# Two more Strassen pairs in each half of both down projections, and what is moved to make room for them

## The chip, the core and the metric

The kernel runs on one core of one Trainium2 chip. The core has a matrix engine (TensorE, PE in the profile), three engines for elementwise work (VectorE or DVE, ScalarE or ACT, GpSimd or POOL, the last unused here) and the SyncE queue (SP), which issues nearly every DMA. The metric is the device time of one execution in microseconds; the median of several runs counts. The profile is of one execution.

## The reference, cut to what matters

```python
# two layers; x is 256 tokens x 2048, all float32; D_FF = 5632
h = rms_norm(x, p['mix_pre'])
m = mixer(h)                                   # attention, differs by layer
x = x + rms_norm(m, p['mix_post'])
h = rms_norm(x, p['ffn_pre'])
x = x + rms_norm(conv_glu(h, *p['ffn']), p['ffn_post'])

def rms_norm(x, g):
    return x * lax.rsqrt(jnp.mean(x * x, axis=-1, keepdims=True) + 1e-6) * g

def conv_glu(h, w_up, conv_w, conv_b, w_down):
    u = h @ w_up                               # 2048 -> 2 x 5632
    gate, val = u[..., :D_FF], u[..., D_FF:]
    gate = depthwise_conv3(gate, conv_w, conv_b)
    return (gelu(gate) * val) @ w_down         # 5632 -> 2048
```

The change touches the channel mixer (`conv_glu`) of both layers and the norm behind it.

## The kernel before

**Products.** TensorE takes operands in a rounded 32-bit format (`fp32r`). To keep float32 accuracy every operand is split into a high part, rounded, and a low part, the rest. A weight chunk is 128 x 1024 (512 KB). It is loaded into a buffer `raw` by SP, its high part `whi` is cast by ScalarE (L157 in `_split`), its low part `wlo` is subtracted by VectorE (L152). A product is high x high, high x low and low x high, three matmuls. `weights()` hands out the chunks in the order of one list for the whole program (`all_chunks`). Of `whi` and `wlo` there are five buffers each, of `raw` four, and `self.more` can name other free tiles that serve as further raw buffers (`raw_more`).

**Stages of the channel mixer** (`ffn`). The up projection runs over eleven groups `gi` of 512 gate columns (`pg`) and 512 value columns (`pv`), eight chunks each. The pre-norm's factor per token, `r`, is not applied to the input but to the results: `self.rb` holds it for all tokens, gates are multiplied by it in `gates`, values by L1140. The product of the gated activation and the value is split into `gh[gi]`, `gl[gi]`. The last group's pair is called `g_last`.

**Down projection** (`down`). Output columns are cut into two halves `h` of 1024. The 5632 rows are 22 pairs of 256. A pair is a 2 x 2 block product (two row blocks, two column blocks, two token blocks of 128). A "plain" pair computes its eight block products, in two chunks of four. A "seven" pair uses Strassen's scheme (Winograd's form): seven block products from sums of weight blocks and sums of token blocks, in units `j` = 0 to 3 that have 2, 2, 2 and 1 products. Units 0 and 3 read the weights as they are (512 KB and 256 KB), units 1 and 2 read sums of weight blocks.
- `PAIRS` says how many of the 22 pairs of each half are "seven": 9 and 11 in both layers.
- `down_order` writes the order of units: `LEAD` plain chunks first, then the seven pairs, with a plain chunk wherever its tuple has `None`, then the plain chunks that are left.
- `block_sums` makes the weight sums during the up projection: it loads a pair's 1 MB from `w_down`, subtracts on VectorE (L1151) and stores the result to DRAM (`self.blocks`), one pair per 7 ticks.
- `sums` makes the token sums of the seven pairs when the down projection begins: five additions on VectorE (L1183) and a split (L692 on ScalarE, L693 on VectorE) for one pair, or for two at once. Results live in tiles that are free by then (`homes`). Both halves use the same token sums.
- `x` is needed again only by the residual, so it is stored (`kept`) in the up projection and loaded back by `x_back` at the end of half 1.
- `done` and `three` make the sums of squares for the norm behind; `crossing` (layer 0) or `tail` (layer 1) ends the stage. The last five plain chunks of half 1 (`HELD`) run first for token block 0, then for block 1, so that the norm of block 0 overlaps with products.

**What sets the order.** A generator such as `block_sums` or `sums` is a background task: `tick()` runs one step of each, and it is called once per chunk. The program so written is then put in order per engine by the scheduler of the framework, which adds the waits; an engine executes in that order. SP, too, is one queue: a DMA that waits for a buffer holds up those behind it.

Of the kernel before, what the change touches and what calls it, by code (L numbers as in the profile page):

```python
# [34 lines left out]

PAIRS = (9, 11), (9, 11)
LEAD = 5, 1


def down_order(h, pairs):

    plain = [("plain", p, o) for o in range(2) for p in range(pairs, KF // 2)]
    out, plain = plain[:LEAD[h]], deque(plain[LEAD[h]:])
    for p in range(pairs):
        for j in (0, None, 1, 2, 3) if h and p > 2 else (0, None, 1, 2, None, 3):
            out.append(plain.popleft() if j is None else ("seven", p, j))
    return out + list(plain)

# [8 lines left out]
class Model:  # L59
# [288 lines left out]
    def pre_norm(self, sp=None):  # L348

        nc = self.nc  # L350
        yield
        ss = self.small.tile([P, 2, 4], F32, tag="ss", name="ss", bufs=2)
        for c in range(4):
            while self.led <= 2 * c:
                yield
            for t in range(2):
                with self.behind(self.gate):
                    self.square_sums(ss[:, t, c:c + 1], self.x[c][:, t, :])
            yield
# [71 lines left out]
        self.nc.sync.dma_start(out=gb, in_=self.a["post"][post:post + 1, 512 * c:512 * c + 512].broadcast_to([P, 512]))  # L431
        return gb

    def three(self, ss):

        part = self.col("part", 2)
        self.nc.vector.tensor_reduce(out=part, in_=ss[:, :, 0:3], op=ALU.add, axis=AX.X)
        self.nc.vector.tensor_scalar(out=part, in0=part, scalar1=1.0 / D, scalar2=EPS, op0=ALU.mult, op1=ALU.add)
        return part

    def factor(self, t, sums, part, after=()):
# [648 lines left out]
    def ffn(self, layer, pre):  # L1090
        nc, tc = self.nc, self.tc
        with tc.tile_pool(name=f"ffn{layer}", bufs=1) as sp:
            self.room = sp
            xs = self.xhl
            x = lambda k: xs[k // 4][:, k % 4].rearrange("p a t -> p (a t)")
            gh = [sp.tile([P, 4, T], F32R, tag=f"gh{i}", name=f"gh{i}") for i in range(NFG - 1)]
            gl = [sp.tile([P, 4, T], F32R, name=f"gl{i}") for i in range(NFG - 1)]
# [5 lines left out]
            blocks = None  # L1103
            for gi in range(NFG):
                if gi == 1:
                    kept = self.dram.tile([4, P, 2, 512], F32, name=f"x_kept{layer}")
                    for c in range(4):
                        nc.sync.dma_start(out=kept[c], in_=self.x[c])
                    blocks = self.now(self.block_sums(layer, sp))
# [19 lines left out]

                if gi:  # L1130
                    gates()
                pv = self.proj_t(KD, x, "at", after=None if gi else gates)
                if gi == NFG - 1:
                    self.finish(blocks)
                    both = sp.tile([P, 2, 4, T], F32R, tag="g_last", name="g_last", bufs=1)
                    gh.append(both[:, 0])
                    gl.append(both[:, 1])
                for i in range(4):
                    u = self.joined(gw[:, 2 + i % 2], misc[:, 2 + i % 2], pv[i])
                    nc.vector.tensor_tensor(out=u, in0=u, in1=self.rb, op=ALU.mult)  # L1140
                    nc.vector.tensor_tensor(out=u, in0=u, in1=act[:, i], op=ALU.mult)
                    self.parted(gh[gi][:, i, :], gl[gi][:, i, :], u)
            self.down(gh, gl, 2 * layer + 1, pre, kept)

    def block_sums(self, layer, sp):

        nc, w = self.nc, self.a[f"w_down{layer}"]
        jobs = [(h, p) for h in range(2) for p in range(PAIRS[layer][h])]

        def minus(x, a, b, n=512):  # L1150
            nc.vector.tensor_tensor(out=x[:, a:a + n], in0=x[:, b:b + n] if n > 512 else x[:, a:a + n],  # L1151
                                    in1=x[:, a:a + n] if n > 512 else x[:, b:b + n], op=ALU.subtract)

        def half(x, i):
            return x[:, 1024 * i:1024 * i + 1024]

        old = None
        for n in range(len(jobs) + 1):
            job, new = (jobs[n] if n < len(jobs) else None), None
            for q in range(7):  # L1160
                if job and q == 0:
                    new = sp.tile([P, 2048], F32, tag=("st", "g_last")[n % 2], name="blocks", bufs=1)
                if job and q < 2:
                    nc.sync.dma_start(out=half(new, q), in_=half(w[job[0], job[1]], q))
                if old and q == 1:
                    with self.behind([self.low]):
                        minus(old[1], 512, 1024, 1024)
                if old and q == 2:
                    with self.behind([self.low]):
                        minus(old[1], 1536, 512)  # L1170
                        minus(old[1], 0, 1536)
                    kept = self.blocks[layer, *old[0]] = self.dram.tile([P, 2048], F32, name=f"b{layer}{old[0][0]}_{old[0][1]}")
                if old and q in (3, 4):
                    nc.sync.dma_start(out=half(kept, q - 3), in_=half(old[1], q - 3))
                    if q == 4 and not job:
                        return
                yield
            old = (job, new)

    def down(self, gh, gl, post, pre, kept):  # L1180

        nc = self.nc
        add = lambda out, a, b, op=ALU.add: nc.vector.tensor_tensor(out=out, in0=a, in1=b, op=op)  # L1183
        mm = nc.tensor.matmul
        ss = self.small.tile([P, 2, 4], F32, tag="ss", name="ss", bufs=2)
        seven, m, gains = [], [], []
        many = PAIRS[0 if pre else 1]

        homes = [(self.act, "x0", 1), (self.act, "x1", 1), (self.act, "xm0", 2), (self.act, "xm1", 2),
                 (self.act, "xm2", 2), (self.room, "st", 2), (self.room, "gw", 1)]  # L1190
        self.more = [(self.act, "x2"), (self.room, "yf"), (self.act, "x3"), (self.room, "misc")]

        def x_back():
            for c in range(4):
                self.x[c] = self.act.tile([P, 2, 512], F32, name=f"x{c}")
                nc.sync.dma_start(out=self.x[c], in_=kept[c])

        def sums(upto, small=False):

            while len(seven) < upto:  # L1200
                p = len(seven)
                pool, tag, q = homes.pop(0)
                k = slice(2 * (p % 2), 2 * (p % 2) + 2 * q)
                if small:
                    tmp = self.wp.tile([P, 2, 512], F32, tag="raw", name="sums", bufs=4)
                else:
                    tmp = self.act.tile([P, 2, 512 * q], F32, tag="xm3", name="sums")
                add(tmp[:, 0], gh[p // 2][:, k].rearrange("p k t -> p (k t)").bitcast(F32),
                    gl[p // 2][:, k].rearrange("p k t -> p (k t)").bitcast(F32))
                a = tmp[:, 0].rearrange("p (q k t f) -> p q k t f", q=q, k=2, t=2)  # L1210
                s = tmp[:, 1].rearrange("p (q n f) -> p q n f", q=q, n=4)
                a11, a12, a21, a22 = (a[:, :, k, t] for t in range(2) for k in range(2))
                add(s[:, :, 0], a21, a22)
                add(s[:, :, 1], s[:, :, 0], a11, ALU.subtract)
                add(s[:, :, 2], a11, a21, ALU.subtract)
                add(s[:, :, 3], a12, s[:, :, 1], ALU.subtract)
                yield
                home = pool.tile([P, q, 4, 2, P], F32R, tag=tag, name=f"seven{p}")
                self.parted(home[:, :, :, 0, :], home[:, :, :, 1, :], s)
                seven.extend(home[:, i] for i in range(q))  # L1220
                yield

        def tokens(k, t):
            return tuple(g[k // 4][:, k % 4, t * P:(t + 1) * P] for g in (gh, gl))
# [44 lines left out]
                yield  # L1269

        gains.append(self.gain_row(post, 0))
        self.now(sums(many[0]))
        ended = None
        for h in range(2):
            items = down_order(h, many[h])
# [46 lines left out]
            if h == 0:  # L1322
# [152 lines left out]
```

## Time and profile before

| | us |
|---|---|
| median of 3 runs | 2039.87 (2039.24 to 2040.02) |
| the profiled execution | 2040.39 |
| its span, first to last instruction | 2038.6 |
| up projection, layer 0 and layer 1 | 342.5 to 820.0, 1326.4 to 1803.8 |
| down projection, layer 0 and layer 1 | 820.1 to 1047.1, 1804.0 to 2029.9 |
| VectorE busy in the up projections | 376 and 377 of 477 |
| VectorE busy in the down projections | 179 of 224 and 178 of 226 |
| DMA share in the same four stages | 0.82, 0.84, 0.82, 0.80 |
| TensorE clock granted | 0.999 |

A line of a group reads: line of the kernel, engine, operation, tiles written and read, shape, count; busy time and mean duration of one; idle time before them and what ended it. Matmuls overlap in the pipeline, so their durations add up to more than the time that passes; the distance from start to start is what one of them takes of the stage. In the table by windows a row has the stretch, the busy time of each engine with its number of instructions, the granted clock, the share of the DMA engines that was busy, and GB/s.

### The profile page before, as it was taken

The page shows a single profiled execution, that of the slowest core. Times are in us where ns is not written, and L with a number is a line of the kernel's source. Part 1 is how long each engine was busy: PE and PEld are TensorE (multiplying, and loading weights), DVE is VectorE, ACT ScalarE, POOL GpSimd, SP SyncE. Part 2 cuts the span into 40 slices and gives each one's busy share as a digit, 9 for nine tenths or more (in the row PEclk, how much of TensorE's full clock was granted, in tenths as well). Part 3 has the DMA queues.
Part 4 walks back from the last instruction along what each step waited for, and adds up shares of the span by engine and source line. Part 5 has one row for each costly group of instructions (what it writes and reads, how often), then busy time and mean ns, then how long its engine had stood idle before and what let it go on. Part 6 is the DMA issues. An engine that isn't in the chain of part 4 may idle for free.

```text
span 2038.6 us, 29774 instructions
## 1 busy us (share of the span) xinstructions
PE 2026.6 (99%) x10882; PEld 1740.7 (85%) x10882; DVE 1562.0 (77%) x2388; ACT 1161.4 (57%) x1817; POOL 0.2 (0%) x4
## 2 busy tenths in 40 slices
PE   9999999999999999999999999999999999999998
PEld 7888888888888888888878998888888888888886
DVE  6877757887887787967787875678887887788777
ACT  7655546655555555656665665565555555566664
POOL 0000000000000000000000000000000000000000
PEclk9999999999999999999999999999999999999999
DMA  9545567788888886788964445688878879768895
GB/s 336 177 152 165 166 196 237 237 312 294 289 314 294 288 293 216 247 292 282 319 220 161 140 128 172 204 277 279 302 272 322 298 278 318 235 200 307 269 318 200
DMA packets 145586, 509.75 MB, mean 250 GB/s; under 512 B 16160, under 2 KB 16672, under 8 KB 145440
## 3 DMA queue, kind: packets, MB, share of 16 engines
q1 hardware_dynamic: 145152, 507.58, 73.9%
q8 instruction: 85, 1.39, 0.3%
q14 instruction: 61, 0.50, 0.1%
q10 hardware_dynamic: 288, 0.28, 0.0%
HBM read 459.55 MB, written 48.23 MB: 249 GB/s over the span
## 4 chain that ended last, share of the span: by engine, by line
PE 98%; DVE 1%; ACT 1%; DMA 1%; issue 0%; DVEq 0%; SPq 0%; ACTq 0%
PE ps L234 31%; PE ps L236 16%; PE ps L219 8%; PE ps L217 8%; PE ps L218 8%; PE ps L1298 7%; PE ps L1299 7%; PE ps L1301 7%; PE ps L644 2%; PE ps L303 1%; PE ps L547 1%; DMA raw<-in_w_in 1%; PE ps L474 0%; PE ps L554 0%; ACT whi L157 0%
## 5 line engine op out<-in xcount | busy, mean ns | idle before, releaser
L152 DVE TENSOR_TENSOR wlo<-raw,whi 128x1024 fp32r<-128x1024 f32 (+1 forms) x655 | 784.3, 1205 | 352.2 <-ACT whi L157 344.3
L157 ACT CAST whi<-raw 128x1024 fp32r<-128x1024 f32 (+1 forms) x655 | 676.8, 1037 | 565.6 <-PE ps L234 280.1
L234 PE MATMUL ps<-xhl,whi 128*128 128x512 f32 x2752 | 952.6, 394 | 0.0
L236 PE MATMUL ps<-xhl,wlo 128*128 128x256 f32 x2752 | 757.5, 277 | 0.0
L234 PEld LDWEIGHTS ps<-xhl,whi 128*128 128x128 f32 x2752 | 513.9, 188 | 117.3
L236 PEld LDWEIGHTS ps<-xhl,wlo 128*128 128x128 f32 x2752 | 516.4, 188 | 2.6
L152 DVE TENSOR_TENSOR wlo<-raw_more,whi 128x1024 fp32r<-128x1024 f32 (+1 forms) x125 | 140.3, 1137 | 55.1 <-ACT whi L157 51.1
L1298 PE MATMUL ps<-whi,gh 128*128 128x512 f32 x440 | 171.3, 389 | 0.0
L1299 PE MATMUL ps<-whi,gl 128*128 128x512 f32 x440 | 171.2, 389 | 0.0
L157 ACT CAST whi<-raw_more 128x1024 fp32r<-128x1024 f32 (+1 forms) x125 | 121.5, 984 | 83.5 <-PE ps L1299 69.3
L1301 PE MATMUL ps<-wlo,gh 128*128 128x512 f32 x440 | 138.7, 389 | 0.0
L217 PE MATMUL ps<-whi,xhl 128*128 128x512 f32 x336 | 132.4, 395 | 0.8 <-ACT whi L157 0.8
L218 PE MATMUL ps<-wlo,xhl 128*128 128x512 f32 x336 | 131.3, 391 | 0.0
L219 PE MATMUL ps<-whi,xhl 128*128 128x512 f32 x336 | 131.0, 391 | 0.1
L1151 DVE TENSOR_TENSOR blocks<-blocks 128x512 f32<-128x512 f32 (+1 forms) x120 | 103.7, 864 | 0.7
L217 PE MATMUL ps<-whi,oh 128*128 128x512 f32 x256 | 100.3, 392 | 0.0
L218 PE MATMUL ps<-wlo,oh 128*128 128x512 f32 x256 | 99.7, 390 | 0.0
L219 PE MATMUL ps<-whi,ol 128*128 128x512 f32 x256 | 99.7, 389 | 0.0
L1298 PEld LDWEIGHTS ps<-whi,gh 128*128 128x128 f32 x440 | 82.6, 188 | 17.6 <-DVE ps L1183 0.4
L1301 PEld LDWEIGHTS ps<-wlo,gh 128*128 128x128 f32 x440 | 82.6, 188 | 17.1
L1299 PEld LDWEIGHTS ps<-whi,gl 128*128 128x128 f32 x440 | 82.6, 188 | 17.0
L307 ACT COPY gw<-ps 128x256 f32<-128x256 f32 x176 | 64.4, 369 | 46.0 <-PE ps L234 28.8
(231 smaller groups left out, 2333.6 us busy)
## 6 DMA issues: line engine op xcount, KB each, us to landing
raw<-in_w_up SPq DMA_DIRECT2D x352, 512.0 KB, 5.1
raw<-in_w_in SPq DMA_DIRECT2D x84, 512.0 KB, 4.2
blocks<-in_w_down SPq DMA_DIRECT2D x80, 512.0 KB, 6.0
b<-blocks SPq DMA_DIRECT2D x80, 512.0 KB, 5.6
raw<-in_w_down SPq DMA_DIRECT2D x77, 512.0 KB, 5.3
raw<-in_w_out SPq DMA_DIRECT2D x64, 512.0 KB, 4.1
raw_more<-in_w_down SPq DMA_DIRECT2D x59, 512.0 KB, 5.7
raw<-b SPq DMA_DIRECT2D x42, 512.0 KB, 5.9
```

The costliest lines, as they stand in the source:

```text
L152: return nc.vector.tensor_tensor(out=lo[:, s], in0=raw[:, s], in1=hi[:, s].bitcast(F32), op=ALU.subtract)
L157: self.nc.scalar.copy(hi[:, s], raw[:, s])
L217: mm(ps, lh, rh, start=start, stop=False)
L218: mm(ps, lh, rl, start=False, stop=False)
L219: return mm(ps, ll, rh, start=False, stop=stop)
L234: ins = mm(out[i], hi[:, s[kk]], x(k), start=k == 0, stop=False, skip_group_check=opening)
L236: ins = mm(out[i][:, :T], lo[:, s[kk]], x(k)[:, :T], start=False, stop=k == nk - 1, skip_group_check=opening)
L307: self.nc.scalar.copy(b, ps[:, T:])
L1151: nc.vector.tensor_tensor(out=x[:, a:a + n], in0=x[:, b:b + n] if n > 512 else x[:, a:a + n], in1=x[:, a:a + n] if n > 512 else x[:, b:b + ...
L1298: mm(bank, xh, w[0][:, c], start=start, stop=False, skip_group_check=loose)
L1299: mm(bank, xl, w[0][:, c], start=False, stop=False, skip_group_check=loose)
L1301: ins = mm(bank, xh, w[1][:, c], start=False, stop=stop, skip_group_check=loose)
```

## The change

The numbers of seven pairs rise from 9 and 11 to 11 and 13, in both layers, and with them the rules of `down_order`. The weight sums start half a group earlier and take 6.8 ticks per pair. The token sums of the first four pairs are made in the up projection, into `x0` to `x3`; eight pairs follow when the down projection starts, the thirteenth in half 1. Three tiles serve as `raw_more`, not four. The values are no longer multiplied by `r`: the norm behind is invariant to a factor per token but for its epsilon, which is multiplied by `v`, the inverse square of that factor (`floor`).

```diff
-PAIRS = (9, 11), (9, 11)
-LEAD = 5, 1
+PAIRS = (11, 13), (11, 13)
+LEAD = 4, 1
+DENSE = (4, 6, 7, 8, 9, 10), (4, 6, 8)
...
     for p in range(pairs):
-        for j in (0, None, 1, 2, 3) if h and p > 2 else (0, None, 1, 2, None, 3):
+        for j in (0, None, 1, 2, 3) if h == 0 and p in DENSE[0] else (0, 1, 2, 3) if p in DENSE[1] and h else \
+                (0, None, 1, 2, 3) if h else (0, None, 1, 2, None, 3):
             out.append(plain.popleft() if j is None else ("seven", p, j))
...
+        self.floor = self.col("floor", 2)
+        nc.vector.tensor_scalar(out=self.floor, in0=v, scalar1=EPS, scalar2=None, op0=ALU.mult)
...
-    def three(self, ss):
+    def three(self, ss, floor=None):
...
+            self.nc.vector.scalar_tensor_tensor(out=part, in0=part, scalar=1.0 / D, in1=floor,
+                                                op0=ALU.mult, op1=ALU.add)
...
+            homes = [(self.act, f"x{c}", 1) for c in range(4)] + [(self.act, f"xm{c}", 2) for c in range(3)] + \
+                [(sp, "st", 2), (self.act, "x0", 1)]
+            sums = lambda upto, *tmp: self.token_sums(seven, homes, gh, gl, upto, *tmp)
             for gi in range(NFG):
+                if gi == 2:
+                    early = self.now(sums(4, sp, "gh9"))
...
-                    nc.vector.tensor_tensor(out=u, in0=u, in1=self.rb, op=ALU.mult)
...
+        todo = {}
+        for n, (h, p) in enumerate(jobs):
+            for at, step in ((0, "load0"), (1, "load1"), (7, "sums"), (8, "keep0"), (9, "keep1")):
+                todo.setdefault(n * 34 // 5 + at, []).append((step, h, p, n))
...
+    def token_sums(self, seven, homes, gh, gl, upto, room, room_tag, bufs=1, pause=6):
...
+            seven.extend(home[:, i] for i in range(q))
+            for _ in range(pause):
+                yield
...
-        homes = [(self.act, "x0", 1), (self.act, "x1", 1), (self.act, "xm0", 2), (self.act, "xm1", 2),
-                 (self.act, "xm2", 2), (self.room, "st", 2), (self.room, "gw", 1)]
-        self.more = [(self.act, "x2"), (self.room, "yf"), (self.act, "x3"), (self.room, "misc")]
+        self.more = [(self.room, t) for t in ("yf", "gw", "misc")]
...
-        self.now(sums(many[0]))
+        self.now(sums(12, self.act, "xm3"))
...
+                if h and i == units[20]:
+                    self.now(sums(many[1], self.wp, "raw", 4))
...
-                self.now(sums(many[1], True))
-        part = self.three(ss)
+        part = self.three(ss, self.floor)
```

Three places show how instructions move.

On TensorE, pair 9 of half 0 in layer 0 is plain before. This is the first of its two chunks, the first of the down projection: token block 0, then block 1, each two products of three matmuls (`gh_3124` and `gl_3134` are `gh[4]` and `gl[4]`, whose last two of four rows are the pair; x2 is two in a row).

```order
L1298 MATMUL ps<-whi,gh_3124 128x512
L1299 MATMUL ps<-whi,gl_3134 128x512
L1298 MATMUL ps<-whi,gh_3124 128x512
L1299 MATMUL ps<-whi,gl_3134 128x512
L1301 MATMUL ps<-wlo,gh_3124 128x512 x2
L1298 MATMUL ps<-whi,gh_3124 128x512
L1299 MATMUL ps<-whi,gl_3134 128x512
L1298 MATMUL ps<-whi,gh_3124 128x512
L1299 MATMUL ps<-whi,gl_3134 128x512
L1301 MATMUL ps<-wlo,gh_3124 128x512 x2
```

Now the same pair is a seven pair further back in half 0. These are its units 2 and 3 (`seven_8306` holds the token sums of pairs 8 and 9).

```order
L1312 MATMUL ps<-whi,seven_8306 128x512
L1313 MATMUL ps<-whi,seven_8306 128x512
L1312 MATMUL ps<-whi,seven_8306 128x512
L1313 MATMUL ps<-whi,seven_8306 128x512
L1315 MATMUL ps<-wlo,seven_8306 128x512 x2
L1312 MATMUL ps<-whi,seven_8306 128x512
L1313 MATMUL ps<-whi,seven_8306 128x512
L1315 MATMUL ps<-wlo,seven_8306 128x512
```

A plain chunk is 12 matmuls and a pair 24; units 0 to 2 are 6 matmuls and unit 3 is 3, a pair 21.

On VectorE, at the start of layer 0's down projection before: token sums of pairs 2 to 5 stand between the splits of the weights.

```order
L1183 TENSOR_TENSOR sums<-gh_3121,gl_3131 128x1024
L152 TENSOR_TENSOR wlo<-raw_more,whi 128x1024
L1183 TENSOR_TENSOR sums<-sums 128x2x128 x3
L152 TENSOR_TENSOR wlo<-raw_more,whi 128x512
L1183 TENSOR_TENSOR sums<-sums 128x2x128
L152 TENSOR_TENSOR wlo<-raw_more,whi 128x1024
L693 TENSOR_TENSOR seven_8144<-sums,seven_8144 128x8x128
L152 TENSOR_TENSOR wlo<-raw,whi 128x1024
L1183 TENSOR_TENSOR sums<-gh_3122,gl_3132 128x1024
L152 TENSOR_TENSOR wlo<-raw,whi 128x1024
```

Now, at the same place: the sums of pairs 6 to 9 (pairs 0 to 3 have been made in the up projection, 4 and 5 just before these rows).

```order
L1198 TENSOR_TENSOR sums<-gh_3125,gl_3134 128x1024
L1198 TENSOR_TENSOR sums<-sums 128x2x128
L154 TENSOR_TENSOR wlo<-raw_more,whi 128x1024
L1198 TENSOR_TENSOR sums<-sums 128x2x128 x3
L154 TENSOR_TENSOR wlo<-raw_more,whi 128x1024
L154 TENSOR_TENSOR wlo<-raw_more,whi 128x512
L701 TENSOR_TENSOR seven_8207<-sums,seven_8207 128x8x128
L1198 TENSOR_TENSOR sums<-gh_3126,gl_3135 128x1024
L154 TENSOR_TENSOR wlo<-raw,whi 128x1024 x2
L1198 TENSOR_TENSOR sums<-sums 128x2x128
```

The start of the stage keeps four double sums; the two single ones that stood ahead of them are gone.

On SP, at the end of half 1 in layer 0, before: `x0` and `x1` are back already, the last plain chunks are loaded, then `x2` and `x3`, then the last held chunk and the next stage's weights.

```order
L135 DMA raw_more_9630<-in_w_down0 128x512
L135 DMA raw_more_9642<-in_w_down0 128x1024
L135 DMA raw_more_9660<-in_w_down0 128x1024
L135 DMA raw_9715<-in_w_down0 128x1024
L135 DMA raw_9727<-in_w_down0 128x1024
L135 DMA raw_9747<-in_w_down0 128x1024
L135 DMA raw_9759<-in_w_down0 128x1024
L1196 DMA x2_9739<-x_kept0_3681 128x1024
L1196 DMA x3_9741<-x_kept0_3681 128x1024
L135 DMA raw_9779<-in_w_down0 128x1024
L135 DMA raw_9819<-in_w_in1 128x1024
```

Now all four loads of `x` stand here. `x0` is the home of the thirteenth pair, so its load waits for that pair's last matmul.

```order
L137 DMA raw_more_9690<-in_w_down0 128x512
L137 DMA raw_9708<-in_w_down0 128x1024
L137 DMA raw_9747<-in_w_down0 128x1024
L137 DMA raw_9765<-in_w_down0 128x1024
L137 DMA raw_9777<-in_w_down0 128x1024
L1235 DMA x1_9787<-x_kept0_3689 128x1024
L1235 DMA x2_9789<-x_kept0_3689 128x1024
L1235 DMA x3_9791<-x_kept0_3689 128x1024
L137 DMA raw_9797<-in_w_down0 128x1024
L1235 DMA x0_9785<-x_kept0_3689 128x1024
L137 DMA raw_9809<-in_w_down0 128x1024
L137 DMA raw_9829<-in_w_down0 128x1024
```

The last three held chunks are behind loads of `x`, where only the last one was.

More of the change, by code (lines that the diff above doesn't have):

```diff
@@ L432, in gain_row @@
         return gb
-    def three(self, ss):
+    def three(self, ss, floor=None):
         part = self.col("part", 2)
         self.nc.vector.tensor_reduce(out=part, in_=ss[:, :, 0:3], op=ALU.add, axis=AX.X)
-        self.nc.vector.tensor_scalar(out=part, in0=part, scalar1=1.0 / D, scalar2=EPS, op0=ALU.mult, op1=ALU.add)
+        if floor is None:
+            self.nc.vector.tensor_scalar(out=part, in0=part, scalar1=1.0 / D, scalar2=EPS, op0=ALU.mult, op1=ALU.add)
+        else:
+            self.nc.vector.scalar_tensor_tensor(out=part, in0=part, scalar=1.0 / D, in1=floor,
+                                                op0=ALU.mult, op1=ALU.add)
         return part
@@ L1131, in ffn @@
                     gates()
+                else:
+                    blocks = self.now(self.block_sums(layer, sp))
                 pv = self.proj_t(KD, x, "at", after=None if gi else gates)
@@ L1137, in ffn @@
                     gl.append(both[:, 1])
+                elif gi == NFG - 2:
+                    for g, n in ((gh, "gh"), (gl, "gl")):
+                        g.append(sp.tile([P, 4, T], F32R, tag=f"{n}{gi}", name=f"{n}{gi}", bufs=1))
                 for i in range(4):
                     u = self.joined(gw[:, 2 + i % 2], misc[:, 2 + i % 2], pv[i])
-                    nc.vector.tensor_tensor(out=u, in0=u, in1=self.rb, op=ALU.mult)
                     nc.vector.tensor_tensor(out=u, in0=u, in1=act[:, i], op=ALU.mult)
                     self.parted(gh[gi][:, i, :], gl[gi][:, i, :], u)
-            self.down(gh, gl, 2 * layer + 1, pre, kept)
+            self.finish(early)
+            self.down(gh, gl, 2 * layer + 1, pre, kept, seven, sums)
     def block_sums(self, layer, sp):
@@ L1155, in half @@
             return x[:, 1024 * i:1024 * i + 1024]
[L1157 to L1165, printed above, removed]
-                    with self.behind([self.low]):
[L1167 to L1176, printed above, removed]
+        todo = {}
@@ new lines, in block_sums @@
+        for n, (h, p) in enumerate(jobs):
+            for at, step in ((0, "load0"), (1, "load1"), (7, "sums"), (8, "keep0"), (9, "keep1")):
+                todo.setdefault(n * 34 // 5 + at, []).append((step, h, p, n))
+        raw = {}
+        for at in range(max(todo) + 1):
+            for step, h, p, n in sorted(todo.get(at, []), key=lambda x: x[3]):
+                if step == "load0":
+                    raw[n] = sp.tile([P, 2048], F32, tag=("st", "g_last")[n % 2], name="blocks", bufs=1)
+                if step[:4] == "load":
+                    nc.sync.dma_start(out=half(raw[n], int(step[4])), in_=half(w[h, p], int(step[4])))
+                elif step == "sums":
+                    with self.behind([self.low]):
+                        minus(raw[n], 512, 1024, 1024)
+                        minus(raw[n], 1536, 512)
+                        minus(raw[n], 0, 1536)
+                    self.blocks[layer, h, p] = self.dram.tile([P, 2048], F32, name=f"b{layer}{h}_{p}")
+                else:
+                    nc.sync.dma_start(out=half(self.blocks[layer, h, p], int(step[4])), in_=half(raw[n], int(step[4])))
+            yield
@@ new lines, in token_sums, with add @@
+    def token_sums(self, seven, homes, gh, gl, upto, room, room_tag, bufs=1, pause=6):
+        def add(out, a, b, op=ALU.add):
+            self.nc.vector.tensor_tensor(out=out, in0=a, in1=b, op=op)
+        while len(seven) < upto:
+            p = len(seven)
+            pool, tag, q = homes.pop(0)
+            k = slice(2 * (p % 2), 2 * (p % 2) + 2 * q)
+            tmp = room.tile([P, 2, 512 * q], F32, tag=room_tag, name="sums", bufs=bufs)
+            add(tmp[:, 0], gh[p // 2][:, k].rearrange("p k t -> p (k t)").bitcast(F32),
+                gl[p // 2][:, k].rearrange("p k t -> p (k t)").bitcast(F32))
+            a = tmp[:, 0].rearrange("p (q k t f) -> p q k t f", q=q, k=2, t=2)
+            s = tmp[:, 1].rearrange("p (q n f) -> p q n f", q=q, n=4)
+            a11, a12, a21, a22 = (a[:, :, k, t] for t in range(2) for k in range(2))
+            add(s[:, :, 0], a21, a22)
+            add(s[:, :, 1], s[:, :, 0], a11, ALU.subtract)
+            add(s[:, :, 2], a11, a21, ALU.subtract)
+            add(s[:, :, 3], a12, s[:, :, 1], ALU.subtract)
+            yield
+            home = pool.tile([P, q, 4, 2, P], F32R, tag=tag, name=f"seven{p}")
+            self.parted(home[:, :, :, 0, :], home[:, :, :, 1, :], s)
+            seven.extend(home[:, i] for i in range(q))
+            for _ in range(pause):
@@ L1177, in block_sums, with down @@
                 yield
-            old = (job, new)
-    def down(self, gh, gl, post, pre, kept):
+    def down(self, gh, gl, post, pre, kept, seven, sums):
         nc = self.nc
@@ L1196, in x_back @@
                 nc.sync.dma_start(out=self.x[c], in_=kept[c])
[L1198 to L1221, printed above, removed]
         def tokens(k, t):
```

9 lines of the change are left out of this document (4 added, 5 removed).

## The prediction

> **What bounds the kernel now.** First the page: how busy the engines are, and the chain of work that ended last.
>
> ```profile
> PE 2026.6 (99%) x10882; PEld 1740.7 (85%) x10882; DVE 1562.0 (77%) x2388; ACT 1161.4 (57%) x1817; POOL 0.2 (0%) x4
> ...
> PE 98%; DVE 1%; ACT 1%; DMA 1%; issue 0%; DVEq 0%; SPq 0%; ACTq 0%
> ```
>
> TensorE is busy for 2026.6 of 2038.6 us, and the chain is 98% TensorE. A busy engine could still be a stretched one, so next its waits, longest first, all that there are:
>
> ```profile
> PE ps L201 <- DVE zeros L1365: 1.1, 1, 1.1
> PE ps L303 <- issue: 0.9, 1, 0.9
> PE ps L217 <- ACT whi L157: 0.8, 1, 0.8
> PE ps L474 <- DVE x L466: 0.6, 2, 0.3
> ```
>
> That is 3.4 us, none of it inside an up or down projection. So the kernel is bound by the number of matmuls and the pace at which they start. The pace comes from the timeline of a stretch of half 0 in layer 0, where a plain chunk (from 881.31) is followed by a unit 3 (from 884.03):
>
> ```profile
> 881.31 0.39 PE L1298 MATMUL ps<-whi,gh 128*128 128x512 f32 x1
> ...
> 882.67 0.39 PE L1298 MATMUL ps<-whi,gh 128*128 128x512 f32 x1
> ...
> 884.03 0.39 PE L1298 MATMUL ps<-whi,seven 128*128 128x512 f32 x1
> 884.26 0.39 PE L1299 MATMUL ps<-whi,seven 128*128 128x512 f32 x1
> 884.48 0.39 PE L1301 MATMUL ps<-wlo,seven 128*128 128x512 f32 x1
> 884.71 0.39 PE L1298 MATMUL ps<-whi,gh 128*128 128x512 f32 x1
> ```
>
> One matmul lasts 0.39 us, but they overlap: the chunk's 12 take 884.03 - 881.31 = 2.72 us and the unit's 3 take 0.68 us, so each costs 0.227 us of the stage. What could bound the kernel next are VectorE (80% busy in the down projections, by the front's table) and the DMA (0.80 to 0.84).
>
> **TensorE's term.** A plain pair is 24 matmuls, a seven pair 21: 5.45 us against 4.77. Eight pairs change kind (two in each half, two halves, two layers): 8 x 3 x 0.227 = **5.45 us less**. Nothing else is taken from or added to TensorE: the order shows 24 matmuls fewer in all. This row bounds the pace:
>
> ```profile
> L1298 PEld LDWEIGHTS ps<-whi,gh 128*128 128x128 f32 x440 | 82.6, 188 | 17.6 <-DVE ps L1183 0.4
> ```
>
> A weight load takes 188 ns beside the matmul ahead of it. If the loads set the pace the term would be 24 x 0.188 = 4.5 us; if a matmul's own 0.389 us did, 9.3 us. The spacing lies between and is measured directly, so I take 5.45.
>
> The Trainium skill, "TensorE: Matmul & The Clock Gate", section "Back-to-back issue gap", gives for a stream of matmuls of 512 columns a sustained 131 ns each and for an isolated gap N/2.4 + 2.5, about 216 ns; with these the term would be an estimated 3.1 or 5.2 us. The measured spacing of 227 ns is above both, and the sum goes by it.
>
> **VectorE in the up projections.** Of each form one row (window: layer 0's up projection, and for the sums layer 1's down projection):
>
> ```profile
> L1151 DVE TENSOR_TENSOR blocks<-blocks 128x512 f32<-128x512 f32 x40 | 27.5, 687 | 0.3
> L1151 DVE TENSOR_TENSOR blocks<-blocks 128x1024 f32<-128x1024 f32 x20 | 24.4, 1218 | 0.0
> L1140 DVE TENSOR_TENSOR misc<-misc 128x256 f32<-128x256 f32 x40 | 15.0, 418 | 0.0
> ...
> L1183 DVE TENSOR_TENSOR sums<-sums 128x256 f32<-128x256 f32 x16 | 6.0, 415 | 0.0
> L1183 DVE TENSOR_TENSOR sums<-gh,gl 128x1024 f32<-128x1024 f32 x4 | 4.9, 1216 | 0.0
> L693 DVE TENSOR_TENSOR seven<-sums,seven 128x1024 fp32r<-128x1024 f32 x4 | 4.9, 1214 | 0.0
> L693 DVE TENSOR_TENSOR seven<-sums,seven 128x512 fp32r<-128x512 f32 x3 | 2.1, 688 | 0.7 <-ACT seven L692 0.7
> L1183 DVE TENSOR_TENSOR sums<-sums 128x128 f32<-128x128 f32 x8 | 2.0, 285 | 0.0
> ```
>
> Per layer: four more jobs of weight sums at 1.22 + 2 x 0.69 = 2.6 us make +10.4. Four single token sums (0.69 + 4 x 0.29 + 0.69 = 2.5 us) make +10.1. The multiplication of 44 values goes: 44 x 0.418 = -18.4. So +2 us on 376 of 477. Cost: nothing, hidden by TensorE's 477 us of products. `floor` is one tiny instruction per layer; in `three` one form replaces another.
>
> **VectorE in the down projections.** A double sum is 1.22 + 4 x 0.415 + 1.21 = 4.1 us. Before: four doubles and three singles, 24 us; after: four and one, 19 us. The splits grow: a plain pair has two chunks of 1.22 us, a seven pair 3.5, so four pairs add 4 x 1.9 = 7.6 us. Net +2.5 on 178 us, while the stage loses 2.7 of 224. What matters is where the work stands. At the start of the stage it is thickest:
>
> ```profile
> 844.00:856.00 12.00, 12.00 (x55) 9.93 (x54) 12.00 (x18) 8.55 (x11) 0.00 (x0) 1.00 0.80 255
> 856.00:868.00 12.00, 12.00 (x55) 9.93 (x54) 12.00 (x15) 7.54 (x8) 0.00 (x0) 1.00 0.84 275
> ```
>
> VectorE (the fourth column) is full for 24 us and TensorE still never waits. Two of the sums that made it so leave this place, which has more room afterwards. The thickest place after is pairs 4, 6 and 8 of half 1, which have no plain chunk: 3 x 1.22 + 0.69 = 4.35 us of splits in 4.77 us. With five `whi` buffers a cast may start when TensorE leaves the chunk five before, so at least four chunks, 4.77 us, remain for a cast and a split (about 2.3 us): 2.5 us to spare. The thirteenth pair's sum (2.5 us) falls on pair 5, which has a plain chunk. I take nothing; between a loss of nothing and 2.5 us per layer.
>
> **DMA in half 1.** A seven pair loads 3.5 chunks of 0.524 MB: 1.84 MB in 4.77 us. Before, from pair 3 on with one plain chunk each, 2.36 MB in 7.49 us is 315 GB/s. After, pairs 3 to 12 are 22.0 MB in 66.7 us, 330 GB/s, and pairs 4 to 8 are 10.2 MB in 29.3 us, 349 GB/s. What the engines moved in half 1 at such demand, and the most in a down projection:
>
> ```profile
> 1948.00:1960.00 12.00, 12.00 (x55) 9.94 (x54) 8.40 (x9) 7.13 (x9) 0.00 (x0) 1.00 0.96 341
> 1960.00:1972.00 12.00, 12.00 (x55) 9.94 (x54) 8.28 (x8) 7.29 (x8) 0.00 (x0) 1.00 0.93 298
> 1972.00:1984.00 12.00, 12.00 (x55) 9.94 (x54) 9.58 (x9) 7.43 (x9) 0.00 (x0) 1.00 0.95 316
> ...
> 1860.00:1872.00 12.00, 12.00 (x55) 9.94 (x54) 8.14 (x8) 5.91 (x7) 0.00 (x0) 1.00 1.00 391
> ```
>
> 391 GB/s at a share of 1.00 says that 349 can be had. The cushion is thinner, though. Raw buffers fall from eight to seven, and a chunk passes every 1.36 us in place of 1.5. From the split that frees a buffer to the cast that needs it again there were 8 x 1.5 - 2.3 = 9.7 us; there are 7 x 1.36 - 2.3 = 7.2, and loads take:
>
> ```profile
> raw<-b SPq DMA_DIRECT2D x42, 512.0 KB, 5.9
> raw_more<-b SPq DMA_DIRECT2D x38, 512.0 KB, 6.1
> ```
>
> So 1.1 us of cushion, and behind it the 2.5 us of the split: 3.6 us in all. I take nothing, and price the other end among the rivals.
>
> **The end of half 1.** SP's queue and the last seven matmuls (layer 0):
>
> ```profile
> 1021.36 4.48 SPq L1196 DMA_DIRECT2D x<-x_kept  x2
> 1026.88 0.33 SPq L135 DMA_DIRECT2D raw<-in_w_down  x1
> 1028.61 13.63 SPq L135 DMA_DIRECT2D raw<-in_w_in  x7
> ...
> 1026.54 0.24 PE ps L1299
> 1026.78 0.67 DVE m L1183
> 1027.45 1.14 DVE wlo L152
> 1028.61 5.30 DMA raw<-in_w_in
> ```
>
> The seven matmuls end at about T = 1026.8. The new wait is `x0`'s, on TensorE, until T; behind it on SP are the last two held chunks, then the next stage's weights. Before, only the last chunk was issued at T, the other at T - 6 or earlier. The first is needed after two plain and three half chunks: T + 9.5. Issued at T + 0.5, landing 5.3 to 6.1 us later, cast and split in 2.3, it is ready at about T + 8.5 to 9, and the last one a microsecond later with its need at T + 10.9. So it just fits. The additions to `x` come after T + 12. I take nothing; bounds: 2 us late in each layer, or 1 us gained where the crossing's waits (0.8 + 0.6 above) shrink.
>
> **Sum.** 2040.39 - 5.45 = 2034.9 for an execution like the profiled one, span about 2033.2. The median of before is 0.5 below its profiled run, so the forecast is 2039.87 - 5.45 = **2034.4 us**.
>
> **Rivals.**
> - *Held chunks late.* The `x0` wait delays the last two chunks beyond their slack; TensorE then waits near the end of each half 1. For it: the slack is below 1 us. Against it: before's last chunk was issued as late and cost nothing. 1 to 2 us per layer: 2036.4 to 2038.4.
> - *DMA cannot keep up in half 1, and the kernel gets slower.* Place: pairs 3 to 12. At rate B the 22.0 MB take 22.0/B; TensorE loses what exceeds 66.7 + 3.6 us. At the lowest row, 298 GB/s, 73.9 us: 3.6 us per layer, 2034.4 + 7 = 2041.5. To be slower by over 0.2% it has to lose 4.8 us per layer: below 293 GB/s. For it: shares of 0.93 to 0.96 already. Against it: 391 at 1.00, and 298 was all that was asked there.
> - *The term is mis-sized.* Pace of the weight loads: 2035.4. The matmul's duration: 2030.5. Both contradict the spacing. The skill's 131 ns would give 2036.7; a plain chunk of 12 would then last 1.6 us, and the trace has 2.72.
> - *The change doesn't do what it says.* 24 matmuls must be gone; the order shows that they are. If sums came late, a seven unit would wait for them: any loss up to the whole gain, 2039.9.
>
> **How the numbers follow.** What a measurement of this kernel can tell from no change is about 0.2%, 4.1 us: faster means below 2035.8, slower above 2043.9. Forecast, nothing else of weight: 0.64, faster. Held chunks: 0.14, of which 0.02 still faster. DMA: 0.13, of which 0.06 slower. Crossing shrinks, to 2033.4: 0.04, faster. A larger term 0.02, faster; a smaller one or no effect 0.03, same. Faster 0.72, same 0.22, slower 0.06. The range from 2033.2 to 2038.5 holds the forecast, the held chunks, the crossing and the milder half of the third; what is left out is 0.06 of slower, some 0.05 around 2039 to 2043, and 0.02 below.
>
> **What would show it.** Right: seven matmuls x192 per line for x160 and `gh` ones x400 for x440; TensorE's waits as before, about 3.4 us; down projections 2.7 us shorter each, up projections unchanged; 533 MB moved in place of 510 (8 x 2.88 MB). Wrong: TensorE waiting for ScalarE's casts in half 1, with the casts waiting for DMA (the rival in the middle of the half) or for the last `raw` loads (the rival at its end); or VectorE's sums named as releaser. The forecast is wrong if those waits pass 1.4 us in all.

## The result and the profile after

| | before | changed |
|---|---|---|
| median, us | 2039.74 (4 runs) | 2051.34 (2050.45 to 2051.62, 4 runs) |
| ratio, 95% interval | | 1.0056 (1.0039 to 1.0074) |
| span of the profiled execution, us | 2038.6 | 2049.3 |

The changed kernel is slower by 11.6 us, 16.9 us above the forecast. (Medians below leave out one execution each of `b6_ffn256`, `b8_ffn192` and `d1_x1`, which took 2510, 5249 and 2877 us.) First its page: the engines and the DMA.

```profile
PE 2036.2 (99%) x10858; PEld 1733.9 (85%) x10858; DVE 1577.9 (77%) x2368; ACT 1176.5 (57%) x1837; POOL 0.2 (0%) x4
...
DMA packets 152499, 532.83 MB, mean 260 GB/s; under 512 B 16928, under 2 KB 17440, under 8 KB 152352
```

There are 24 matmuls fewer (10858 for 10882), and 533 MB as foretold. Yet TensorE is busy for 9.6 us longer. All waits of TensorE, longest first, and the groups of the down projections' first line:

```profile
PE ps L305 <- issue: 1.3, 1, 1.3
PE ps L203 <- DVE zeros L1380: 1.1, 1, 1.1
PE ps L219 <- ACT whi L159: 0.9, 1, 0.9
PE ps L1312 <- ACT whi L159: 0.7, 1, 0.7
PE ps L482 <- DVE x L474: 0.3, 1, 0.3
```

```profile
L1312 PE MATMUL ps<-whi,gh 128*128 128x512 f32 x400 | 158.7, 397 | 0.9 <-ACT whi L159 0.7
L1312 PE MATMUL ps<-whi,seven 128*128 128x512 f32 x192 | 75.3, 392 | 0.0
```

The waits come to 4.3 us, for 3.4 before, and only the 0.7 us lie in a down projection. The counts are the foretold ones (400 and 192). So TensorE has less to do, and its waits explain 0.9 us at most: it must be slower per matmul. The stages, from the start of the first to that of the last matmul of each:

| us | before | changed | difference |
|---|---|---|---|
| start to layer 0's up projection | 330.3 | 332.4 | +2.1 |
| up projection, each layer (with its first products ahead) | 489.7 | 489.6 | -0.1 |
| down projection, layer 0 | 227.0 | 229.6 | +2.6 |
| from there to layer 1's up projection | 267.1 | 268.9 | +1.9 |
| down projection, layer 1 | 225.9 | 230.2 | +4.3 |

Even the mixers, whose program was not changed, are slower, and the up projections are not. The granted clock is 0.999 in both. The timeline of TensorE in the changed kernel, half 0 of layer 0, shows where the time goes: a unit 3 of a seven pair and the plain chunk behind it.

```profile
882.08 0.39 PE L1312 MATMUL ps<-whi,seven 128*128 128x512 f32 x1
...
882.76 0.40 PE L1312 MATMUL ps<-whi,gh 128*128 128x512 f32 x1
...
885.56 0.40 PE L1312 MATMUL ps<-whi,gh 128*128 128x512 f32 x1
```

This unit's three matmuls take 882.76 - 882.08 = 0.68 us, 227 ns each, as before (not all units do, as is told below). The chunk's twelve take 2.80 us, 233 ns each, for 2.72 before. No wait stands between them, and the matmul's own 0.39 us hardly moves. The two differ in their stationary operand, `seven` here and `gh` there. These lie in different pools, and the pool of `gh` has moved, as the built programs show:

```
byte address in a partition          before    changed
xhl0 (first pool)                      4352       4352
whi, first of five                    69888      69888
floor, two buffers                        -     112224, 112256
gh0 (pool of the stage)              117504     117568
```

`floor` is a new tile of two columns with two buffers, 32 bytes each. It stands ahead of the pool of each stage, and so all tiles of the mixers and the channel mixer start 64 bytes further on. The seven pairs' sums lie mostly in the first pool, where `x` and the norm's input were.

### The profile page after: what moved, and what is told of

It reads as the page before. It is cut to its first block, busy times and chain, and to the rows that moved or that the text cites. A ratio compares the mean times of both kernels' runs of the same rounds, so it can differ in the third digit from the quotient of the medians.

```text
span 2049.3 us, 29865 instructions
## 1 busy us (share of the span) xinstructions
PE 2036.2 (99%) x10858; PEld 1733.9 (85%) x10858; DVE 1577.9 (77%) x2368; ACT 1176.5 (57%) x1837; POOL 0.2 (0%) x4
## 4 chain that ended last, share of the span: by engine, by line
PE 96%; DVE 1%; DMA 1%; ACT 1%; issue 0%; DVEq 0%; SPq 0%; ACTq 0%
PE ps L236 31%; PE ps L238 15%; PE ps L221 8%; PE ps L219 8%; PE ps L220 8%; PE ps L1312 7%; PE ps L1315 7%; PE ps L1313 7%; PE ps L652 1%; PE ps L305 1%; PE ps L555 1%; DVE wlo L154 1%; DMA raw<-in_w_in 0%; ACT whi L159 0%; PE ps L482 0%; PE ps L562 0%
## 5 line engine op out<-in xcount | busy, mean ns | idle before, releaser
L154 DVE TENSOR_TENSOR wlo<-raw,whi 128x1024 fp32r<-128x1024 f32 (+1 forms) x681 | 809.9, 1198 | 356.9 <-ACT whi L159 354.6
L159 ACT CAST whi<-raw 128x1024 fp32r<-128x1024 f32 (+1 forms) x681 | 698.7, 1030 | 605.2 <-PE ps L236 298.8
L1312 PE MATMUL ps<-whi,gh 128*128 128x512 f32 x400 | 158.7, 397 | 0.9 <-ACT whi L159 0.7
L154 DVE TENSOR_TENSOR wlo<-raw_more,whi 128x1024 fp32r<-128x1024 f32 (+1 forms) x115 | 129.1, 1139 | 38.0 <-ACT whi L159 37.8
L1313 PE MATMUL ps<-whi,gl 128*128 128x512 f32 x400 | 157.7, 394 | 0.0
L159 ACT CAST whi<-raw_more 128x1024 fp32r<-128x1024 f32 (+1 forms) x115 | 111.0, 981 | 64.0 <-PE ps L1313 41.1
L1315 PE MATMUL ps<-wlo,gh 128*128 128x512 f32 x400 | 129.8, 396 | 0.1
L1168 DVE TENSOR_TENSOR blocks<-blocks 128x1024 f32<-128x1024 f32 x144 | 124.4, 864 | 0.9
L1312 PEld LDWEIGHTS ps<-whi,gh 128*128 128x128 f32 x400 | 75.1, 188 | 19.9 <-ACT whi L159 1.7
L1315 PEld LDWEIGHTS ps<-wlo,gh 128*128 128x128 f32 x400 | 75.0, 188 | 18.7 <-DVE wlo L154 0.8
```

Source lines behind the costliest of these rows:

```text
L154: return nc.vector.tensor_tensor(out=lo[:, s], in0=raw[:, s], in1=hi[:, s].bitcast(F32), op=ALU.subtract)
L159: self.nc.scalar.copy(hi[:, s], raw[:, s])
L1312: mm(bank, xh, w[0][:, c], start=start, stop=False, skip_group_check=loose)
L1313: mm(bank, xl, w[0][:, c], start=False, stop=False, skip_group_check=loose)
L1315: ins = mm(bank, xh, w[1][:, c], start=False, stop=stop, skip_group_check=loose)
```

## The experiments

In what follows *stationary* is the 128 x 128 operand that LDWEIGHTS brings, *moving* the operand that streams past it. In the down projections a part of `gh`, `gl` or `seven` is stationary and the weight chunk (`whi`, `wlo`) moves. In the up projections it is the other way round. d is the start of the stationary operand less that of the moving one, modulo 256 bytes; in the kernel before, d is 0 for all 10544 matmuls with 256 or 512 columns.

### Does the place of the tiles do it?

`c1_floor_in_r` keeps `floor` but puts it where no tile moves:

```diff
-        self.r = self.col("prer", 2)
+        both = self.col("prer", 4)
+        self.r, self.floor = both[:, :2], both[:, 2:]
...
-        self.floor = self.col("floor", 2)
```

> The changed kernel, floor kept as it is computed, but in the two unused columns of the tile of r, so that no tile moves: the stages' pool starts at 117504 again. Address theory: down spacing 227 ns, 2051.34 - 2376 x 6.6 ns = about 2035.6. Rival theory (floor's own work, the other form in the norm, or the removed multiplication changes TensorE's pace): 2050 or so, as the changed kernel.

Measured: 2037.82 us, 2.78 less than the kernel before in the same session (ratio 0.9988, 0.9979 to 0.9997). In its timeline a plain chunk takes 2.72 us again:

```profile
885.91 0.39 PE L1312 MATMUL ps<-whi,gh 128*128 128x512 f32 x1
...
888.63 0.39 PE L1312 MATMUL ps<-whi,seven 128*128 128x512 f32 x1
```

So the place of `floor` cost 11.60 + 2.78 = 14.4 us, and its work nothing that shows. It is 2.2 us above what the address theory gave; that is taken up below.

`b1_pad64` does only the harm: the kernel before, with an unused tile.

```diff
+        self.small.tile([P, 16], F32, tag="pad", name="pad", bufs=1)
```

> The kernel before with one unused tile of 64 bytes among the small columns, nothing else. Address theory: 2520 matmuls of 512 columns read weights from the shifted pool, x 6.6 ns = 16.6 us more, about 2056.5, and spacing 233 in place of 227 ns in the down projections. Rival theory (the order or the load of the change is the cause): as before, 2039.9.

Measured: 2054.30, 14.6 us more than before (ratio 1.0072, 1.0060 to 1.0085), with no instruction added. The plain chunk takes 2.80 us:

```profile
888.07 0.39 PE L1299 MATMUL ps<-whi,gh 128*128 128x512 f32 x1
...
890.87 0.39 PE L1299 MATMUL ps<-whi,gh 128*128 128x512 f32 x1
```

`a2_rb` takes `floor` out altogether and multiplies the values by `rb` again.

```diff
-        self.floor = self.col("floor", 2)
-        nc.vector.tensor_scalar(out=self.floor, in0=v, scalar1=EPS, scalar2=None, op0=ALU.mult)
...
+                    nc.vector.tensor_tensor(out=u, in0=u, in1=self.rb, op=ALU.mult)
...
-        part = self.three(ss, self.floor)
+        part = self.three(ss)
```

> The changed kernel without floor: the values are multiplied by the factor again (44 x 0.418 = 18.4 us of VectorE per layer in the up projections), the norm behind is as before. The pool stands where it stood. Address theory: about 2035.6 as with the pad, unless VectorE's 18 us show (397 of 477 busy, so at most a few us). Rival theory (the additional seven pairs are the cause): 2051 or more.

Measured: 2037.79, 1.9 less than before (ratio 0.9990, 0.9981 to 0.9999). The seven pairs and their sums alone don't slow the kernel down; the rival falls here too.

### Which offsets cost?

Two more pads: 128 bytes in all in the changed kernel (`a1_pad128`, an unused tile of 16 columns beside `floor`), and 32 bytes in the kernel before (`b2_pad32`, the diff of `b1_pad64` with 8 columns).

> The changed kernel with one unused tile of 64 bytes more among the small columns, nothing else: floor (two buffers of 32 bytes) shifted every tile of the stages' own pool from a start at a multiple of 128 bytes to 64 bytes past one; with the pad they are 128 bytes past the old place. Address theory (a matmul of 512 columns costs 6.6 ns more when its 128x128 weights start 64 bytes past a multiple of 128): the spacing of such matmuls in the down projections goes back from 232-233 to 227 ns, and the time falls by 2376 x 6.6 ns = 15.7 us to about 2035.6; what is left over 2034.4 are waits. If the unit is 256 bytes, nothing changes: 2051. Rival theory (the denser order, the DMA or the sums slow TensorE down): no change, 2051.

> The kernel before with an unused tile of 32 bytes, so that the stages' pool starts 32 bytes past a multiple of 64. Address theory: if any start that isn't a multiple of 128 costs the same, about 2056.5 as with 64 bytes; if the cost goes with the bytes past the line or only the half line matters, between 2040 and 2056; a start off 64 bytes may cost twice, 2073. Rival theory: 2039.9.

Measured: 2049.62 (ratio 1.0049, 1.0037 to 1.0062) and 2054.01 (1.0070, 1.0057 to 1.0084). I had expected 128 bytes to heal it, and they don't: 12.7 us more than `c1_floor_in_r`, each against its own runs of before. 32 bytes cost about as much as 64.

Then the question whether a place is bad in itself. `b3_all64` moves every tile by 64 bytes; `b6_ffn256` moves the channel mixer's pool alone by 256.

```diff
+        self.const.tile([P, 16], F32, name="pad")
```

```diff
+            sp.tile([P, 64], F32, name="pad")
             gh = [sp.tile([P, 4, T], F32R, tag=f"gh{i}", name=f"gh{i}") for i in range(NFG - 1)]
```

> The kernel before with 64 bytes ahead of all tiles, so that weights and moving operands of every matmul start 64 bytes past a multiple of 256, all alike. If it is where the 128x128 weights start that costs: 6728 matmuls of 512 columns x 6.6 ns, 44 us more, 2084, and the 512-column ones of the up projections slow down as well. If only the offset between the two operands of a matmul counts (a collision of their reads): 2039.9 as before.

> The kernel before with 256 unused bytes at the start of the channel mixer's pool alone: gh, gl and g_last move from 256 past a multiple of 512 to a multiple of 512; all else stays. If the unit is 256 bytes: 2039.9, spacing 227 ns. If it is 512 bytes: another pace in the down projections, faster or slower by about 1500 x 6.6 = 10 us.

Measured: 2040.41 (ratio 0.9998, 0.9989 to 1.0008) and 2040.63 (0.9999, 0.9990 to 1.0009): no change in either. With all tiles 64 bytes off the chunk takes 2.72 us:

```profile
884.75 0.39 PE L1299 MATMUL ps<-whi,gh 128*128 128x512 f32 x1
...
887.47 0.39 PE L1299 MATMUL ps<-whi,gh 128*128 128x512 f32 x1
```

My theory that a start off some multiple costs in itself falls: it gave 2084. What counts is the distance between the two operands, modulo 256 bytes.

`e1_wp64` tests this by moving the other operand: the weight chunks (and with them the stages' pool) by 64 bytes, `xhl` not.

```diff
+        self.wp.tile([P, 16], F32, tag="pad", name="pad", bufs=1)
```

> The kernel before with 64 unused bytes ahead of raw, whi and wlo: these and the stages' pool move by 64 bytes, xhl and the other tiles of the first pool don't. If the offset between weights and moving operand counts: the down projections keep 227 ns (gh and whi moved alike, 2520 matmuls unchanged), the other 4208 matmuls of 512 columns (the up projections, where xhl are the weights and whi moves, and the projections of the mixers) cost 6.6 ns more: +27.8 us, 2068, and more if the 2960 of 256 columns pay too. If only the stages' pool's place counts: 2056, the down projections slow, the up projections as before.

(The expectation names the operands of the up projections the wrong way round: there the chunk is stationary and `xhl` moves.) Measured: 2060.19, 19.8 us more (ratio 1.0096, 1.0080 to 1.0111), less than the 27.8 expected. The stages have changed places. The down projection is at its old pace, 2.72 us a chunk, in this kernel:

```profile
884.26 0.39 PE L1299 MATMUL ps<-whi,gh 128*128 128x512 f32 x1
...
886.98 0.39 PE L1299 MATMUL ps<-whi,gh 128*128 128x512 f32 x1
```

And the up projection is not. Ten pairs of a 512- and a 256-column matmul, in the kernel before and then in `e1_wp64`:

```profile
599.95 0.40 PE L234 MATMUL ps<-xhl,whi 128*128 128x512 f32 x1
...
603.41 0.40 PE L234 MATMUL ps<-xhl,whi 128*128 128x512 f32 x1
```

```profile
599.95 0.40 PE L235 MATMUL ps<-xhl,whi 128*128 128x512 f32 x1
...
603.48 0.40 PE L235 MATMUL ps<-xhl,whi 128*128 128x512 f32 x1
```

346 ns a pair become 353. The up projections take 498.4 and 498.3 us for 489.7: 17.3 us / 2752 pairs = 6.3 ns. That leaves about 2.5 us for 1440 matmuls of 512 columns with d = 192, 1.7 ns each. (The expectation of `b8_ffn192` puts all of these in the mixers. But 384 belong to seven pairs whose sums lie in the first pool, and the down projections, first to last matmul, are 0.8 and 0.5 us longer than before.) So the sign seemed to count, and the last run of this group asks for it: `b8_ffn192` is the diff of `b6_ffn256` with 48 columns.

> The kernel before with 192 unused bytes at the start of the channel mixer's pool alone: the stationary gh, gl and g_last start 192 bytes past the moving chunk's place (modulo 256) where the pad of 64 bytes had 64; 1656 matmuls of 512 columns. If any offset costs alike, 5.8 ns each (14.6 us / 2520 with 64 bytes): +9.6 us, about 2050. If the sign counts (with the chunks moved by 64, the mixers' projections, whose stationary operand then starts 192 past, cost 2 to 2.5 ns more only): +3.3 to 4.1 us, about 2044.

Measured: 2045.03, 4.7 us more (ratio 1.0022, 1.0012 to 1.0032): 2.9 ns each, nearer the second case. A chunk takes 2.75 us, 2.3 ns more per matmul:

```profile
885.20 0.39 PE L1299 MATMUL ps<-whi,gh 128*128 128x512 f32 x1
...
887.95 0.39 PE L1299 MATMUL ps<-whi,gh 128*128 128x512 f32 x1
```

All of them together (us against the kernel before; the changed kernel and the pad of 128 against `c1_floor_in_r`, each by its own runs of before; 48 matmuls with the opposite d in the rows of 32 to 192 are left out of count, save that of 128). The fifth column spreads the difference over the counted matmuls. The last one is direct: the same matmul in the two traces, from its start to the next one's start, the mean over those of 512 columns whose own d is not a multiple of 256 (for `b6_ffn256`, over the moved tiles of the down projections):

| d, bytes | kernel | matmuls of 512 columns | us more | ns, spread | ns, direct |
|---|---|---|---|---|---|
| 32 | `b2_pad32` | 2520 | 14.3 | 5.7 | 6.0 |
| 64 | `b1_pad64` | 2520 | 14.6 | 5.8 | 6.3 |
| 64 | changed | 2376 | 14.4 | 6.1 | 6.2 |
| 128 | `a1_pad128` | 2424 | 12.7 | 5.2 | 5.4 |
| 192 | `b8_ffn192` | 1608 | 4.7 | 2.9 | 2.2 |
| 256, so 0 | `b6_ffn256` | 1656 | 0.0 | 0.0 | 0.2 |

The two columns differ because other matmuls change pace as well, which the spread charges to the counted ones. The seven pairs whose sums lie in the first pool keep d = 0 in the first five rows, and yet their matmuls are 2 to 3 ns slower on average, in the midst of matmuls whose tiles moved. A unit 3 of this kind in `b1_pad64` takes 0.70 us, for 0.68:

```profile
887.37 0.39 PE L1299 MATMUL ps<-whi,seven 128*128 128x512 f32 x1
...
888.07 0.39 PE L1299 MATMUL ps<-whi,gh 128*128 128x512 f32 x1
```

And the matmuls of 256 columns outside the up projections are 1.5 to 2.3 ns faster in the first four rows, 1.5 to 2.3 us in all. So d of a matmul's own operands orders the cases, but it does not settle the pace of each single matmul; what else does is open.

### What is left of the change

With the tiles in place the gain is 2.78 of the 5.45 us of the forecast. In layer 1 TensorE waits in the middle of half 1, at pair 6; in the changed kernel this is the 0.7 us of the list above. Three views of that place in the changed kernel, the queue of SP, ScalarE's casts and VectorE's token sums:

```profile
1966.75 2.07 SPq L137 DMA_DIRECT2D raw_more<-b  x2
1970.43 2.06 SPq L137 DMA_DIRECT2D raw<-in_w_down  x3
1972.77 0.33 SPq L137 DMA_DIRECT2D raw<-b  x1
1973.14 0.66 SPq L1235 DMA_DIRECT2D x<-x_kept  x1
1978.80 0.32 SPq L137 DMA_DIRECT2D raw<-b  x1
```

```profile
1970.91 0.62 ACT L159 CAST whi<-raw 128x512 fp32r<-128x512 f32 x1 [0.30 <-ACT whi L159]
1976.47 1.05 ACT L159 CAST whi<-raw 128x1024 fp32r<-128x1024 f32 x1 [4.93 <-DMA raw<-in_w_down]
```

```profile
1965.43 0.69 DVE L1198 TENSOR_TENSOR sums<-gh,gl 128x512 f32<-128x512 f32 x1
...
1970.31 0.69 DVE L701 TENSOR_TENSOR seven<-sums,seven 128x512 fp32r<-128x512 f32 x1
```

The thirteenth pair's sums use a `raw` buffer as scratch, from before 1965.4 until 1971.0. Of the seven buffers for loads one is gone for that time, SP issues one load into `raw` at 1962.8 and the next only at 1970.4, and a cast waits 4.9 us for its load. `d1_x1` gives the sums another scratch, `x1`, whose pair is done by then:

```diff
-                    self.now(sums(many[1], self.wp, "raw", 4))
+                    self.now(sums(many[1], self.act, "x1", 1))
```

> As the run with floor in r's tile, and the thirteenth pair's token sums use x1 (free by then) as scratch in place of one of the four raw buffers. In layer 1 of the changed kernel TensorE waits 0.9 + 0.2 us at pair 6 of half 1 for a cast that waits for a load. Theory A (the scratch holds a raw buffer until its split, so SP's next loads start late): that wait goes, 1 to 1.5 us less than the run beside it. Theory B (the DMA as such falls behind in the dense pairs): the wait stays, no difference.

Measured: 2035.49, 2.33 less than `c1_floor_in_r` beside it and 5.11 less than before (ratio 0.9974, 0.9963 to 0.9984). At the same place no cast waits for a load:

```profile
1957.99 0.62 ACT L159 CAST whi<-raw 128x512 fp32r<-128x512 f32 x1 [0.30 <-PE ps L1313]
1958.90 1.06 ACT L159 CAST whi<-raw 128x1024 fp32r<-128x1024 f32 x1 [0.28 <-PE ps L1313]
```

SP's queue shows the buffer that was missing. At the same point of the order `c1_floor_in_r` (first row) issues one load into `raw`, with none after it until 1957.87, and `d1_x1` (second row) two in a row:

```profile
1950.39 0.33 SPq L137 DMA_DIRECT2D raw<-in_w_down  x1
```

```profile
1950.14 1.69 SPq L137 DMA_DIRECT2D raw<-in_w_down  x2
```

So theory A holds, and theory B falls. (The later load of `x1` moves too, out of this place; no run takes the two apart.) In the profiled executions, 2037.14 and 2035.94 us, it is less: 1.2 us. Of that 0.8 us lie here. In `c1_floor_in_r` TensorE stood still between these two rows, which are 1.06 us apart in place of 0.23:

```profile
1963.72 0.39 PE L1315 MATMUL ps<-wlo,seven 128*128 128x512 f32 x1
1964.78 0.50 PE L1312 MATMUL ps<-whi,gh 128*128 128x512 f32 x1 [0.67 <-ACT whi L159]
```

What else the medians differ by is not placed.

`d3_pairs9_11` is `d1_x1` with the numbers of pairs put back, `PAIRS = (9, 11), (9, 11)`.

> As the run with x1 as scratch, with PAIRS back at 9 and 11, all else of the change kept. The forecast's sum: 24 matmuls more x 0.227 = 5.45 us more, 2041.0. If the rest of the change (spread sums, no multiplication of the values) has a gain or a price of its own, it shows against the kernel before: 2040.6 when it has none.

Measured: 2039.65, 0.79 less than before (ratio 0.9995, 0.9986 to 1.0004, so not told from none). The eight pairs are thus worth about 5.11 - 0.79 = 4.3 us in place of 5.45, from two sessions. In `d3_pairs9_11` TensorE has no wait inside a down projection; `d1_x1` keeps one of 0.6 us, by the starts of its matmuls, at the start of layer 1's (TensorE for a cast). `d2_lead5` was to remove that one by `LEAD = 5, 1`.

> As the run with x1 as scratch, with LEAD back at 5, 1 (five plain chunks ahead of half 0's seven pairs). There TensorE waits 0.6 us at the start of layer 1's down projection for a cast. If the pile of splits and double sums at the start causes it, a plain chunk more ahead lets it shrink: 0 to 0.6 us less. If it is the chunk's own load or the last group's split, no difference: 2035.6.

Measured: 2039.91 (ratio 0.9994, 0.9985 to 1.0002), a miss: the wait was still 0.5 us, and two others grew, at the crossing into layer 1 (0.8 us in `d1_x1`) and in layer 1's mixer (0.5 us there):

```profile
PE ps L482 <- DVE x L474: 2.4, 2, 2.1
PE ps L305 <- issue: 1.6, 1, 1.6
```

At the crossing VectorE takes one more split of a weight chunk between two steps of the norm's factor, so that the additions to `x` start later against TensorE's last products. The order of that short stretch differs from kernel to kernel; why it turned out this way was not followed further. The two waits are 2.7 us of the 4.4 between the medians; the rest is not placed.

## Why the prediction was wrong

- **TensorE's term.** The count was right: 24 matmuls fewer. The step that failed is the sentence "Nothing else is taken from or added to TensorE", with the pace of 0.227 us carried over to the changed kernel. I took that pace for a property of a matmul of its shape, and bounded it by the weight load and the matmul's duration. The runs show that it depends on where the two operands lie: the moved tiles cost 14.4 us, and in the trace the matmuls with d = 64 are 6.2 ns slower each.
- **`floor`.** I called it "one tiny instruction per layer" and priced the instruction. Its price was the 64 bytes of the tile. The same work in a place that moves nothing gives 2037.8.
- **DMA and buffers in half 1.** "I take nothing" was wrong: by 2.33 us in the medians, of which the traces place 0.8 us in this wait. I had set 1.1 us of cushion for seven raw buffers, and set the thirteenth pair's sum down as VectorE work alone; it takes one of these buffers away as well. The wait came where the rival put it, in the dense pairs, but for want of a buffer and not of bandwidth. It appeared in layer 1 alone; why not in layer 0 is open.
- **VectorE.** Foretold: 2 us more in an up projection, hidden. Windows of layer 0's up projection, before and then `c1_floor_in_r`, which has the same order as the changed kernel and the old pace:

```profile
342.50:819.50 477.00, 477.00 (x2756) 417.06 (x2754) 375.65 (x587) 263.70 (x405) 0.00 (x0) 1.00 0.82 282
```

```profile
342.50:819.50 477.00, 477.00 (x2755) 417.27 (x2754) 380.95 (x584) 266.27 (x408) 0.00 (x0) 1.00 0.85 298
...
844.00:856.00 12.00, 12.00 (x55) 9.94 (x54) 11.36 (x14) 7.54 (x8) 0.00 (x0) 1.00 0.86 304
856.00:868.00 12.00, 12.00 (x54) 9.94 (x53) 8.16 (x8) 7.02 (x9) 0.00 (x0) 1.00 0.83 270
```

  It is 5.3 us more, and hidden. Of the 3.3 us above the forecast 1.7 are four of the 44 multiplications, which lay behind this window's end in the kernel before, and 1.0 is the stage's first token sum, which begins inside the window and is a double one now. At the start of the down projection the two full stretches have room now (11.36 and 8.16 of 12), as argued, but in the first it is thin: `d1_x1` has 11.98 there. That layer 1 has a wait there of some 0.6 us was not foreseen.
- **The end of half 1.** No wait in layer 0 from the load of `x0`, so "it just fits" held; the rival of the held chunks fell.
- **The sum.** Forecast 2034.4, measured 2051.3: 14.4 us are the place of the tiles, 2.3 go with the scratch, and 0.3 is what `d1_x1` (-5.11) lacks of the 5.45; from different sessions, they add up to 17.0 for 16.9. That `d1_x1` comes within 0.3 us of the term is in part luck: `d3_pairs9_11` gives 4.3 us for the eight pairs, and the other 0.8 us is the rest of the change, which is not told from none.
- **What would show it.** I had listed waits that would show a wrong step, and none of them could show this one: TensorE did not wait. The view that shows it, the distance from start to start by form of matmul, I had used on the kernel before only to set a price.

## What to carry to other kernels

A tile that is added to a pool moves every tile behind it: compare the addresses of the two operands of the matmuls, modulo 256 bytes, before and after a change, and put small new values into spare columns of a tile that is there. On an engine that is always busy a change of pace leaves no wait; compare the start-to-start distance of the same form of instruction in both traces. A scratch tile taken from a rotation of load buffers counts as one buffer fewer for as long as it is held.

The version that beats both kernels here is `d1_x1`: the change, with `floor` in spare columns and `x1` as scratch, 2035.49 us.

## What the hardware showed that I had not expected

The pace of 512-column matmuls, each with its own weight load, depends on the distance between the starts of stationary and moving operand modulo 256 bytes: about 5 to 6 ns more at 32, 64 and 128 and about 2 at 192, on 227. Where d is 0 throughout nothing is lost, with all tiles moved by 64 bytes or one pool by 256. Nothing in a record of one instruction tells of it: the weight load lasts 188 ns in the changed kernel as before, and the clock is 0.999.

```profile
L1312 PEld LDWEIGHTS ps<-whi,gh 128*128 128x128 f32 x400 | 75.1, 188 | 19.9 <-ACT whi L159 1.7
```

No run here shows the mechanism, nor why the sign counts, why matmuls with d = 0 slow down among others, nor what steps smaller than 32 bytes do.
